# Every reciprocal square root as one GpSimd power, and another order of loads and work in the first norm of an encoder block

## The chip, the core and the metric

The kernel runs on one core of a Trainium2 chip. The metric is the device time of one execution in microseconds; a version's time is the median of its runs. TensorE multiplies matrices, VectorE, ScalarE and GpSimd (POOL in the profile) work on tiles of up to 128 partitions, and SyncE (SP) issues most of the transfers between the device's memory and the on-chip memory (SBUF; the matmul results land in PSUM).

## The reference, cut to what matters

```python
def rmsnorm(t, w, eps=1e-6):
    return t * lax.rsqrt(mean(t * t, -1) + eps) * w
h  = rmsnorm(x, norm1_w)                    # x: 1024 tokens x 1024
p  = h @ w_in                               # q/k/v, z, decay and beta logits, two gates
oa = diff_attention(rope(qa), rope(ka), va) # 8 heads, two softmaxes each, no mask
ya = rmsnorm(oa, subln_w) @ w_proj_attn     # norm over each head's 128 channels
qg, kg, vg = silu(conv5(qkv_g))             # centred, over the tokens
qg, kg = l2norm(qg), l2norm(kg)             # 8 heads of 128
o  = delta_rule(forward) + delta_rule(backward)   # chunks of 64 tokens
yg = (rmsnorm(o, gdn_norm_w) * silu(z)) @ w_proj_gdn
x  = x + (sigmoid(gate_a) * ya + sigmoid(gate_g) * yg) @ w_out
h2 = rmsnorm(x, norm2_w)
x  = x + expert_choice_ffn(h2)              # 16 experts, each takes its top 128 tokens
out = rmsnorm(x, norm_f_w)
```

Every `rsqrt` here, in the three norms, the head norms and the two l2norms, is a root that the change touches. All values are float32.

## The kernel before

The eight tiles of 128 tokens are normed, transposed by TensorE into the blocks `hh` and `hl` (each value as the sum of two that TensorE takes at its fast rate), and then a stream of tasks runs: the logit products of the gated delta rule (GDN below), its eight heads, the eight attention heads, the merge, the router, the sixteen experts, the last norm. Weights come in as float32 and are split the same way, ScalarE casting and GpSimd subtracting.

No order is written out by hand. Tasks are generators that record operations with a helper each: L391 is a product, L395 a transpose (both TensorE), L403 any ScalarE operation, L409, L428, L429 and L434 are VectorE's, L413 and L514 are GpSimd's products and scalar operations, L420 its memset, L483 a transfer. Each record has a planner cost in ns, and `run` takes, again and again, the operation that could start first by the planner's clocks, then by the task's priority. Each engine executes in the order so made. A change of one cost or one operation therefore plans everything behind it anew. Names in the rows are SBUF blocks (A, B, C, W with a number) or `psum`; small vectors lie in the C and B blocks.

A root is `rsqrt` (L528, eleven VectorE operations: an integer seed in two and three Newton steps of three) or, for seven of the eight router tiles, `prsqrt` (L516, two on VectorE and twelve on GpSimd). There are 45: eight of [128x1] in the first norm (`norm_tile`, L719), eight of [128x16] in the GDN heads (`Head.main`, L974), eight of [128x8] at the end of those heads (`Head.finish`, L1173; there the head's output is scaled, transposed and projected) and eight at the end of the attention heads (L1372), eight of [128x1] in the router (L1580), and five at the end: four of [128x2] for pairs of token tiles (`final_pair`, L1947) and one of [128x1] (L1886) for the tile whose rows the scatter waits for.

The first norm (`norm_first`, L753) asks SyncE for the norm's weights, the identity for the transposes and then the eight tiles of x, in that order. The mean square of a tile is a ScalarE square with an accumulator. Even tiles are scaled by root and weight in one VectorE operation, odd tiles by ScalarE (root) and GpSimd (weight). Eight transposes of a tile are evicted by ScalarE (`hh`), and VectorE takes the rest (`hl`, the "residual" below). A task `consts` records the constants' transfers at once, among them the convolution weights, which VectorE scales once.

At the very end the pairs of token tiles are normed while SyncE stores them, and odd tiles of the first three pairs are scaled by ScalarE and GpSimd.

Of the kernel before, what the change touches and what calls it, by code (L numbers as in the profile page):

```python
# [10 lines left out]
I32 = mybir.dt.int32  # L11
# [8 lines left out]
NT = S // P  # L20
# [14 lines left out]
def bcast(ap, shape):  # L35
    return ap.to_broadcast(shape)
# [72 lines left out]
class Emit:  # L109
# [405 lines left out]

    def prsqrt(self, y, x, t):  # L516

        i = t[:, 1].bitcast(I32)
        t = t[:, 0]
        self.ts(i, x.bitcast(I32), 1, op0=ALU.arith_shift_right)  # L520
        self.ts(y.bitcast(I32), i, -1.0, float(0x5F3759DF), op0=ALU.mult, op1=ALU.add)
        for _ in range(3):
            self.ptt(t, y, y, ALU.mult)
            self.ptt(t, t, x, ALU.mult)
            self.pts(t, t, -0.5, 1.5)
            self.ptt(y, t, y, ALU.mult)

    def rsqrt(self, y, x, t):  # L528

        i = t[:, 1].bitcast(I32)  # L530
        t = t[:, 0]
        self.ts(i, x.bitcast(I32), 1, op0=ALU.arith_shift_right)
        self.ts(y.bitcast(I32), i, -1.0, float(0x5F3759DF), op0=ALU.mult, op1=ALU.add)
        for _ in range(3):
            self.tt(t, y, y, ALU.mult)
            self.stt(t, t, -0.5, x, ALU.mult, ALU.mult)
            self.stt(y, t, 1.5, y, ALU.add, ALU.mult)

# [179 lines left out]

def norm_tile(g, st, w1):  # L719
    e = g.e  # L720
    xs = yield from e.new("xs", [P, D])
    e.dma(xs.v, g.ins["x"][st * P:(st + 1) * P, :])
    yield
    ss, rs = g.nsm[:, st:st + 1], g.nsm[:, 8 + st:9 + st]
    e.act(g.jk.v, xs.v, AF.Square, accum_out=ss)
    e.ts(ss, ss, 1.0 / D, 1e-6)
    e.rsqrt(rs, ss, g.nsm[:, 16 + 2 * st:18 + 2 * st].rearrange("p (a b) -> p a b", b=1))
    yield
    if st % 2:
        e.cp(xs.v, xs.v, scale=rs)  # L730
        e.ptt(xs.v, xs.v, w1.v, ALU.mult)
    else:
        e.stt(xs.v, xs.v, rs, w1.v, ALU.mult, ALU.mult)
    pt = yield from e.new("n0", [P, 8, P])
    for d in range(8):
        e.tr(pt[:, d, :], xs[:, d * P:(d + 1) * P], g.ident.v)
    yield
    o = slice(st * P, (st + 1) * P)
    e.cp(g.hh[:, :, o], pt.v)
    e.tt(g.hl[:, :, o], pt.v, f32(g.hh[:, :, o]), ALU.subtract)  # L740
    e.free(xs, pt)

    def done():
        g.tiles.add(st)
        g.hready[0] = g.tiles >= {0, 1, 2, 3}
        g.hready[1] = len(g.tiles) == 8
    e.then(done)
    if st == 7:
        e.free(w1, g.jk)
        e.close("xs", "w1", "n0", "jk")  # L750


def norm_first(g):  # L753
    e = g.e
    g.hT = e.now_new("hh", [P, 8, S], F32R), e.now_new("hl", [P, 8, S], F32R)
    g.hh, g.hl = g.hT[0].v, g.hT[1].v
    g.nsm = e.now_new("nsm", [P, 96]).v
    g.hready, g.tiles = [False, False], set()
    w1 = e.now_new("w1", [P, D])
    g.jk = e.now_new("jk", [P, D])  # L760
    e.spawn(norm_tile(g, 0, w1), 0)
    yield
    e.dma(w1.v, bcast(g.ins["norm1_w"], [P, D]))
    e.dma(g.ident.v, g.ins["c_ident"])
    for st in range(1, NT):
        e.spawn(norm_tile(g, st, w1), 0)
        yield
# [96 lines left out]
class Head:  # L864
# [81 lines left out]
    def main(self):  # L946
# [26 lines left out]
        e.ts(ss, ss, 1e-6, op0=ALU.add)  # L973
        e.rsqrt(rk, ss, rt)  # L974
        e.tt(irk, rk[:, 0:8], ss[:, 0:8], ALU.mult)
# [183 lines left out]
    def finish(self):  # L1159
# [12 lines left out]
        e.ts(m2, m2, 1.0 / 128, 1e-6)  # L1172
        e.rsqrt(rr, m2, rt)  # L1173
        e.tt(rr, rr, aq, ALU.mult)
# [50 lines left out]
class Attn:  # L1225
# [142 lines left out]
    def finish(self):  # L1368
        g, e, o, sm = self.g, self.g.e, self.o, self.sm
        ss, rr = sm[:, 0:8], sm[:, 8:16]  # L1370
        e.ts(ss, ss, 1.0 / 128, 1e-6)
        e.rsqrt(rr, ss, sm[:, 16:32].rearrange("p (a b) -> p a b", b=8))  # L1372
        e.tt(o.v, o.v, bcast(rr[:, :, None], [P, NT, P]), ALU.mult)
# [181 lines left out]
def router(g, st, xt, po):  # L1555
# [23 lines left out]
    e.ts(ss, ss, 1.0 / D, 1e-6)  # L1579
    (e.rsqrt if st == NT - 1 else e.prsqrt)(rs, ss, sm[:, 4:6].rearrange("p (a b) -> p a b", b=1))  # L1580
    pl = yield from e.new("gp", [P, 512])
# [152 lines left out]
class Experts:  # L1734
# [142 lines left out]
    def last(self, pd):  # L1877
# [7 lines left out]
        e.ts(ss, ss, 1.0 / D, 1e-6)  # L1885
        e.rsqrt(rs, ss, rt.rearrange("p (a b) -> p a b", b=1))  # L1886
        e.stt(x.v, x.v, rs, g.wf.v, ALU.mult, ALU.mult)
# [51 lines left out]
def final_pair(g, st, xs, fs):  # L1939
# [6 lines left out]
    e.ts(ss, ss, 1.0 / D, 1e-6)  # L1946
    e.rsqrt(rs, ss, fs[:, 16 + 2 * st:20 + 2 * st].rearrange("p (a b) -> p a b", b=2))  # L1947
    for i, x in enumerate(xs):
# [34 lines left out]
def body(tc, ins, out, dbg=None, heads=H):  # L1983
# [3 lines left out]
    with ExitStack() as ctx:  # L1987
# [170 lines left out]
```

## Time and profile before

| what | value |
|---|---|
| median of 3 runs | 3042.06 us (3036.37 to 3043.48) |
| the profiled execution | 3041.05 us |
| its span in the trace | 3039.3 us, 40711 instructions |
| TensorE products, weight loads | 2874.6 us (95%), 2401.8 us (79%) |
| VectorE, ScalarE, GpSimd | 2371.7 us (78%), 1752.0 us (58%), 567.5 us (19%) |
| TensorE's granted clock, mean | 0.981 of full speed |

Busy times are shares of the span; the engines work at the same time, so the shares don't add up. What remains of the execution's time beside its span is 1.75 us. Times of rows in the sections below count from the span's start.

### The profile page before, as it was taken

The numbers are of one execution on the slowest core, as the hardware profiler recorded it, in microseconds if no ns is written. First come the engines' busy times: TensorE is split into PE (matmuls) and PEld (weight loads), VectorE is DVE, ScalarE is ACT, GpSimd is POOL, SyncE is SP. The second block draws the span as 40 slices with busy tenths as digits, with TensorE's granted clock in tenths as the row PEclk, the third lists the DMA queues.
The fourth block names the chain that finished last, engine by engine and source line by source line (L and its number), as shares of the span: only waits on it lengthen the run. The fifth ranks groups of instructions, "written<-read, shape, count | busy, mean of one in ns | idle before, by whom it ended". The sixth has DMA issues, their size and how long they took to land.

```text
span 3039.3 us, 40711 instructions
## 1 busy us (share of the span) xinstructions
PE 2874.6 (95%) x14780; PEld 2401.8 (79%) x14780; DVE 2371.7 (78%) x3948; ACT 1752.0 (58%) x2668; POOL 567.5 (19%) x448
## 2 busy tenths in 40 slices
PE   7999999899998999999999997899999999999996
PEld 6787887788787878888888786788888888888884
DVE  7768778777865777777862458899888989989887
ACT  5435445444534666776662323577767777777775
POOL 3222222222212211211216332500000000000001
PEclk9999999999999999999999997899999999999998
DMA  4222322321322111112459736899999999999995
GB/s 139 52 68 83 84 61 60 90 63 52 89 74 61 49 49 49 49 49 56 112 161 290 231 105 246 311 390 378 372 386 381 380 383 377 378 377 381 373 355 235
DMA packets 203642, 598.75 MB, mean 197 GB/s; under 512 B 84384, under 2 KB 102304, under 8 KB 154288
## 3 DMA queue, kind: packets, MB, share of 16 engines
q1 hardware_dynamic: 189856, 562.06, 51.4%
q0 software_dynamic: 13584, 34.08, 4.0%
q8 instruction: 116, 1.90, 0.3%
q14 instruction: 86, 0.70, 0.1%
HBM read 535.19 MB, written 52.49 MB: 193 GB/s over the span
## 4 chain that ended last, share of the span: by engine, by line
PE 70%; DVE 15%; ACT 3%; DMA 3%; issue 3%; SPq 1%; POOL 1%; POOLq 0%; DVEq 0%; ACTq 0%
PE psum L391 66%; DVE B L409 6%; PE psum L395 4%; DVE B L434 4%; ACT B L403 2%; DVE B L451 2%; SPq L483 1%; ACT psum L403 1%; DMA dw<-B 1%; DVE B L428 1%; DVE B L455 0%; POOL W L413 0%; ACT W L403 0%; DMA A<-dh,C 0%; DMA B<-dl 0%
## 5 line engine op out<-in xcount | busy, mean ns | idle before, releaser
L391 PE MATMUL psum<-A,W 128*128 128x512 f32 (+1 forms) x5856 | 1548.6, 404 | 13.8 <-POOL W L413 5.5
L391 PEld LDWEIGHTS psum<-A,W 128*128 128x128 f32 (+1 forms) x5856 | 1068.0, 189 | 213.4 <-DVE A L409 10.2
L391 PE MATMUL psum<-B 128*128 128x128 f32 (+3 forms) x3494 | 651.6, 324 | 15.9 <-DVE B L455 7.6
L391 PEld LDWEIGHTS psum<-B 128*128 128x128 f32 x3494 | 544.8, 191 | 92.4 <-DVE B L455 11.1
L403 ACT ACTIVATE B<-psum 128x512 f32<-128x512 f32 (+4 forms) x612 | 266.4, 441 | 400.4 <-PE psum L395 225.3
L403 ACT ACTIVATE B<-B 128x2048 fp32r<-128x2048 f32 (+4 forms) x341 | 381.8, 1130 | 183.3 <-DVE B L434 80.8
L413 POOL TENSOR_TENSOR W<-W,W 128x1024 fp32r<-128x1024 f32 (+1 forms) x105 | 265.2, 2527 | 945.9 <-ACT W L403 818.1
L409 DVE TENSOR_TENSOR B<-B,B 128x2048 fp32r<-128x2048 f32 (+2 forms) x189 | 377.3, 2006 | 34.0 <-ACT B L403 27.1
L391 PE MATMUL psum<-B,W 128*128 128x512 f32 x1536 | 374.0, 395 | 4.0 <-DVE B L409 3.8
L391 PEld LDWEIGHTS psum<-B,W 128*128 128x128 f32 x1536 | 286.0, 189 | 74.2 <-DVE B L409 14.8
L403 ACT ACTIVATE B<-psum,B 128x128 f32<-128x128 f32 (+2 forms) x264 | 190.9, 728 | 197.4 <-PE psum L391 124.7
L395 PE MATMUL psum<-C,B 128*128 128x128 f32 (+1 forms) x1392 | 218.9, 281 | 71.7 <-DVE B L434 28.3
L409 DVE TENSOR_TENSOR A<-B,A 128x2048 fp32r<-128x2048 f32 x112 | 256.7, 2306 | 15.6 <-ACT A L403 14.5
L391 PE MATMUL psum<-A,B 128*128 128x512 f32 x1024 | 264.5, 398 | 2.3 <-DVE A L409 2.3
L395 PEld LDWEIGHTS psum<-C,B 128*128 128x128 f32 (+1 forms) x1392 | 170.6, 144 | 120.7 <-DVE B L434 35.0
L403 ACT ACTIVATE A<-B 128x2048 fp32r<-128x2048 f32 (+1 forms) x121 | 222.7, 1857 | 41.4 <-PE psum L391 20.6
L391 PE MATMUL psum<-B,B 128*128 128x128 f32 (+1 forms) x1024 | 212.6, 294 | 13.7 <-DVE B L460 11.5
L391 PEld LDWEIGHTS psum<-A,B 128*128 128x128 f32 x1024 | 191.0, 189 | 40.5 <-DVE A L409 3.0
L391 PEld LDWEIGHTS psum<-B,B 128*128 128x128 f32 x1024 | 175.4, 192 | 40.9 <-DVE B L460 14.8
L497 POOL DMA_INDIRECT dx<-B,C x15 | 24.3, 1618 | 953.9 <-ACT B L403 953.9
L451 DVE TENSOR_REDUCE B<-psum 128x1 f32<-128x1024 f32 (+1 forms) x136 | 157.3, 1158 | 53.9 <-PE psum L391 53.0
L413 POOL TENSOR_TENSOR B<-B,B 128x128 f32<-128x128 f32 (+3 forms) x98 | 131.6, 1346 | 308.6 <-ACT B L403 218.8
(116 smaller groups left out, 2852.6 us busy)
## 6 DMA issues: line engine op xcount, KB each, us to landing
B<-in_w_gu_dram SPq DMA_DIRECT2D x154, 1024.0 KB, 7.3
A<-in_w_gu_dram SPq DMA_DIRECT2D x77, 1024.0 KB, 7.3
B<-in_w_dn_dram SPq DMA_DIRECT2D x74, 1024.0 KB, 7.3
A<-in_w_dn_dram SPq DMA_DIRECT2D x40, 1024.0 KB, 7.6
W<-in_w_gu_dram SPq DMA_DIRECT2D x25, 1024.0 KB, 7.1
W<-in_w_gdn_dram SPq DMA_DIRECT2D x32, 512.0 KB, 3.7
B<-dG SPq DMA_DIRECT2D x32, 512.0 KB, 5.6
W<-in_w_proj_dram SPq DMA_DIRECT2D x32, 512.0 KB, 4.6
```

The source lines that it names most:

```text
L391: self.op("pe", c, lambda: self.nc.tensor.matmul(out, lhsT, rhs, start=start, stop=stop), [out], [lhsT, rhs], l, "mm")
L395: self.op("pe", 109, lambda: self.nc.tensor.transpose(out, in_, ident), [out], [in_, ident], 55, "tr")
L403: self.op("act", c, lambda: self.nc.scalar.activation(out, in_, func, **kw), [out] + w, [in_] + r, 0, "act")
L409: self.op("dve", 69 + 1.041 * free(out), lambda: self.nc.vector.tensor_tensor(out, a, b, op), [out], [a, b], 0, "tt")
L413: self.op("pool", 150 + 2.104 * free(out), lambda: self.nc.gpsimd.tensor_tensor(out, a, b, op), [out], [a, b], 0, "ptt")
L428: lambda: (self.nc.vector.tensor_scalar(out, a, s1, None, op0=op0) if s2 is None else self.nc.vector.tensor_scalar(out, a, s1, s2, op0=op0 ...
L434: lambda: self.nc.vector.scalar_tensor_tensor(out, a, s, b, op0=op0, op1=op1),
L451: self.op("dve", 69 + 1.041 * free(in_), lambda: self.nc.vector.tensor_reduce(out, in_, axis=AX.X, op=op), [out], [in_], 0, "red")
L483: self.op("sp", 478, lambda: self.nc.sync.dma_start(out, in_), [out], [in_], 0, "dma", max(n / 360.0, 112))
L497: self.op("pool", 1100, lambda: self.nc.gpsimd.indirect_dma_start(out=dst, out_offset=bass.IndirectOffsetOnAxis(ap=idx, axis=0), in_=y, in ...
```

## The change

`prsqrt` and the old `rsqrt` go. The new `rsqrt` is one GpSimd operation, x to the power of a column that holds -0.5, with a planner cost of 150 + 20n ns for n columns; the column is set once, at the start. The first norm asks for tile 0 of x first, then the identity, the norm's weights and the other tiles; all eight tiles are scaled by VectorE; the constants are asked for only when two tiles are done (by then the logit weights and the first projection weights are in the queue ahead of them).

```diff
-    def prsqrt(self, y, x, t):
...
-    def rsqrt(self, y, x, t):
-        i = t[:, 1].bitcast(I32)
-        t = t[:, 0]
-        self.ts(i, x.bitcast(I32), 1, op0=ALU.arith_shift_right)
-        self.ts(y.bitcast(I32), i, -1.0, float(0x5F3759DF), op0=ALU.mult, op1=ALU.add)
-        for _ in range(3):
-            self.tt(t, y, y, ALU.mult)
-            self.stt(t, t, -0.5, x, ALU.mult, ALU.mult)
-            self.stt(y, t, 1.5, y, ALU.add, ALU.mult)
+    def rsqrt(self, y, x):
+        n = free(x)
+        h = self.half[:, 0:1] if n == 1 else bcast(self.half[:, 0:1], [P, n])
+        self.op("pool", 150 + 20 * n, lambda: self.nc.gpsimd.tensor_tensor(y, x, h, op=ALU.pow), [y], [x, self.half], 0, "pow")
...
-def norm_tile(g, st, w1):
+def norm_tile(g, st, w1, xs):
     e = g.e
-    xs = yield from e.new("xs", [P, D])
-    e.dma(xs.v, g.ins["x"][st * P:(st + 1) * P, :])
-    yield
     ss, rs = g.nsm[:, st:st + 1], g.nsm[:, 8 + st:9 + st]
     e.act(g.jk.v, xs.v, AF.Square, accum_out=ss)
     e.ts(ss, ss, 1.0 / D, 1e-6)
-    e.rsqrt(rs, ss, g.nsm[:, 16 + 2 * st:18 + 2 * st].rearrange("p (a b) -> p a b", b=1))
+    e.rsqrt(rs, ss)
     yield
-    if st % 2:
-        e.cp(xs.v, xs.v, scale=rs)
-        e.ptt(xs.v, xs.v, w1.v, ALU.mult)
-    else:
-        e.stt(xs.v, xs.v, rs, w1.v, ALU.mult, ALU.mult)
+    e.stt(xs.v, xs.v, rs, w1.v, ALU.mult, ALU.mult)
...
     w1 = e.now_new("w1", [P, D])
+    e.pset(e.half, -0.5)
     g.jk = e.now_new("jk", [P, D])
-    e.spawn(norm_tile(g, 0, w1), 0)
-    yield
-    e.dma(w1.v, bcast(g.ins["norm1_w"], [P, D]))
-    e.dma(g.ident.v, g.ins["c_ident"])
-    for st in range(1, NT):
-        e.spawn(norm_tile(g, st, w1), 0)
+    for st in range(NT):
+        xs = yield from e.new("xs", [P, D])
+        e.dma(xs.v, g.ins["x"][st * P:(st + 1) * P, :])
+        if st == 0:
+            e.dma(g.ident.v, g.ins["c_ident"])
+            e.dma(w1.v, bcast(g.ins["norm1_w"], [P, D]))
+        e.spawn(norm_tile(g, st, w1, xs), 0)
         yield
...
         def consts():
+            yield lambda: len(g.tiles) > 1
             for n, shp in (("neg", [P, 2, P]), ("eye16", [P, 256]), ("m16", [P, 2, P]), ("m32", [P, 2, P])):
```

Every other caller only loses the scratch argument.

How the order of the engines moves, at the start and at the last GDN head. On ScalarE at the start, `B_81,C_76<-B_80` is a square of an x tile with its accumulator, `A_78<-psum` the eviction of a tile's transposes, `B_80<-B_80,C_76` the scaling of an odd tile, and `W_111<-W_83` (`W_99` after) the cast of the logit weights (128x256) and of the first projection weights (128x1024). Before:

```order
L403 ACTIVATE B_81,C_76<-B_80 128x1024 x5
L403 ACTIVATE A_78<-psum 128x8x128
L403 ACTIVATE B_80<-B_80,C_76 128x1024
L403 ACTIVATE B_81,C_76<-B_80 128x1024 x2
L403 ACTIVATE A_78<-psum 128x8x128
L403 ACTIVATE B_80<-B_80,C_76 128x1024
L403 ACTIVATE A_78<-psum 128x8x128
L403 ACTIVATE B_81,C_76<-B_80 128x1024
L403 ACTIVATE W_111<-W_83 128x256
L403 ACTIVATE W_111<-W_83 128x1024
```

And after:

```order
L403 ACTIVATE B_81,C_76<-B_80 128x1024 x2
L403 ACTIVATE A_78<-psum 128x8x128
L403 ACTIVATE B_81,C_76<-B_80 128x1024 x2
L403 ACTIVATE A_78<-psum 128x8x128
L403 ACTIVATE B_81,C_76<-B_80 128x1024 x2
L403 ACTIVATE A_78<-psum 128x8x128
L403 ACTIVATE B_81,C_76<-B_80 128x1024
L403 ACTIVATE A_78<-psum 128x8x128
L403 ACTIVATE B_81,C_76<-B_80 128x1024
L403 ACTIVATE W_99<-W_83 128x256
L403 ACTIVATE W_99<-W_83 128x1024
```

The scalings of odd tiles are gone from ScalarE, and four evictions instead of three stand ahead of the logit weights. On TensorE at the same place, L395 `psum<-C_76,B_80` are transposes of x tiles, eight to a tile, and L391 the logit products. Before:

```order
L395 MATMUL psum<-C_76,B_80 128x128 x24
L391 MATMUL psum<-A_78,W_111 32x256
L395 MATMUL psum<-C_76,B_80 128x128 x16
L391 MATMUL psum<-A_79,W_111 32x256
L391 MATMUL psum<-A_78,W_111 32x256 x2
```

And after:

```order
L395 MATMUL psum<-C_76,B_80 128x128 x40
L391 MATMUL psum<-A_78,W_99 32x256
L391 MATMUL psum<-A_79,W_99 32x256
L391 MATMUL psum<-A_78,W_99 32x256 x2
L391 MATMUL psum<-A_79,W_99 32x256
```

Five tiles are transposed ahead of all logit products, where one such product stood among them. On VectorE the scaling of the convolution weights now stands between the scaling of a sixth tile and the fifth tile's residual. The other place is VectorE at the end of the last GDN head (`Head.finish`): the 128x8 rows are the mean square and the root, `B_80<-B_80,B_82 128x1024` the scaling of the head's output, `B_7778<-B_82,B_7778 64x1024` residuals of projection weights (`B_7524` after), and `B_82<-B_82,B_80` and `B_80<-B_80` of 128x1024 belong to attention. Before, from the mean's last step on:

```order
L429 TENSOR_SCALAR B_82<-B_82 128x8
L428 TENSOR_SCALAR B_82<-B_82 128x8
L429 TENSOR_SCALAR B_82<-B_82 128x8
L409 TENSOR_TENSOR B_82<-B_82 128x8
L434 SCALAR_TENSOR_TENSOR B_82<-B_82 128x8
L409 TENSOR_TENSOR B_7778<-B_82,B_7778 64x1024 x2
...
L409 TENSOR_TENSOR B_82<-B_82,B_80 128x1024
L409 TENSOR_TENSOR B_80<-B_80 128x1024
L434 SCALAR_TENSOR_TENSOR B_82<-B_82 128x8
L409 TENSOR_TENSOR B_82<-B_82,B_80 128x1024
...
L409 TENSOR_TENSOR B_80<-B_80,B_82 128x1024
```

And after:

```order
L428 TENSOR_SCALAR B_82<-B_82 128x8
L409 TENSOR_TENSOR B_82<-B_82 128x8 x2
L429 TENSOR_SCALAR B_82<-B_82 128x8
L409 TENSOR_TENSOR B_82<-B_82 128x8
L409 TENSOR_TENSOR B_7524<-B_82,B_7524 64x1024 x2
L409 TENSOR_TENSOR B_80<-B_80,B_82 128x1024
```

The steps of the root and the three attention products between them are gone from the stretch; the two residuals still stand ahead of the scaling.

## Rows read from the trace of the kernel before

**Rows 1.** Stages: us, busy (instructions) PE, PEld, DVE, ACT, POOL; PEclk, DMA share, GB/s.
```profile
0.00:44.70 44.70, 25.40 (x170) 22.37 (x170) 27.59 (x110) 25.49 (x37) 14.66 (x10) 0.92 0.48 164
44.70:960.00 915.30, 863.59 (x4910) 737.43 (x4909) 681.19 (x1973) 408.88 (x1149) 224.45 (x194) 0.99 0.26 71
...
1976.00:2980.00 1004.00, 1003.58 (x4539) 818.83 (x4538) 901.04 (x550) 736.15 (x508) 40.08 (x28) 1.00 0.98 377
2980.00:3040.00 60.00, 31.42 (x129) 24.10 (x127) 44.39 (x83) 27.32 (x31) 10.15 (x4) 0.79 0.52 211
```

**Rows 2.** Timeline, first 13 us: start, us, instruction [idle before, releaser].
```profile
0.75 0.39 SPq L483 DMA_DIRECT2D B<-in_norm_w_dram  x1
...
8.11 1.06 ACT L403 ACTIVATE B<-B 128x1024 f32<-128x1024 f32 x1 [6.09 <-DMA B<-in_x_dram]
...
11.61 1.28 DVE L434 SCALAR_TENSOR_TENSOR B<-B,C 128x1024 f32<-128x1024 f32 x1
...
12.96 1.97 PE L395 MATMUL psum<-C,B 128*128 128x128 f32 x8 [12.96 <-DVE B L434]
```

**Rows 3.** Timeline from 13 us to the first projection (last three: TensorE's alone).
```profile
13.23 0.33 SPq L483 DMA_DIRECT2D C<-in_conv_w_dram  x1
...
14.96 1.02 ACT L403 ACTIVATE A<-psum 128x1024 fp32r<-128x1024 f32 x1 [0.52 <-PE psum L395]
...
17.10 2.36 POOL L413 TENSOR_TENSOR B<-B 128x1024 f32<-128x1024 f32 x1 [16.64 <-ACT B L403]
...
20.62 1.14 ACT L403 ACTIVATE B<-B,C 128x1024 f32<-128x1024 f32 x1
...
21.84 3.24 POOL L413 TENSOR_TENSOR B<-B 128x1024 f32<-128x1024 f32 x1 [2.38 <-ACT B L403]
...
23.60 1.36 ACT L403 ACTIVATE W<-W 128x256 fp32r<-128x256 f32 x2
...
25.18 3.67 PE L395 MATMUL psum<-C,B 128*128 128x128 f32 x16 [0.81 <-DVE C L409]
28.50 5.21 PE L391 MATMUL psum<-A,W 128*32 128x256 f32 x32
...
44.69 9.59 PE L391 MATMUL psum<-A,W 128*128 128x512 f32 x41
```

**Rows 4.** Timeline at the end of the last GDN head.
```profile
973.87 0.17 DVE L429 TENSOR_SCALAR B<-B 128x8 f32<-128x8 f32 x1
...
974.88 2.47 DVE L409 TENSOR_TENSOR B<-B,B 64x1024 fp32r<-64x1024 f32 x2
...
984.39 7.85 DVE L409 TENSOR_TENSOR B<-B,B 128x1024 f32<-128x1024 f32 x3
...
985.67 1.11 PE L395 MATMUL psum<-C,B 128*128 128x128 f32 x4 [8.79 <-DVE B L409]
```

**Rows 5.** TensorE's waits from 76 to 1000 us: total us, times, longest.
```profile
PE psum L395 <- DVE B L409: 19.1, 6, 8.8
```

**Rows 6.** Chain that ended last, from 2985 to 3040 us, by line.
```profile
by line: issue 24.3%; DVE B L409 18.8%; DVE B L434 8.0%; DVE C L434 7.2%; ACT B L403 5.6%; DMA out_dram<-B 4.8%; DVE C L429 3.8%; DVE C L409 3.7%; PE psum L391 2.9%; DVE A L434 2.5%; POOLq L2154 2.2%; DVE C L428 1.3%; PE psum L395 0.8%; DVE
```

**Rows 7.** GpSimd's instructions by form: count | busy us, mean ns | idle before, releasers.
```profile
L413 POOL TENSOR_TENSOR W<-W,W 128x1024 fp32r<-128x1024 f32 x104 | 264.5, 2544 | 945.9 <-ACT W L403 818.1 <-PE psum L391 86.0 <-PE psum L395 27.3
...
L413 POOL TENSOR_TENSOR B<-B 128x1 f32<-128x1 f32 x63 | 12.0, 191 | 67.3 <-DVE B L429 62.8
```

**Rows 8.** Timeline at a router root made on GpSimd.
```profile
1842.66 0.13 DVE L429 TENSOR_SCALAR B<-B 128x1 int32<-128x1 int32 x1
...
1842.93 0.46 POOL L413 TENSOR_TENSOR B<-B 128x1 f32<-128x1 f32 x2 [8.23 <-DVE B L429]
...
1846.13 0.17 DVE L451 TENSOR_REDUCE B<-psum 128x1 f32<-128x16 f32 x1 [0.41 <-PE psum L391]
```

**Rows 9.** Transfers issued in the first 60 us: count, KB each, us to landing.
```profile
B<-in_norm_w_dram SPq DMA_DIRECT2D x1, 512.0 KB, 4.4
...
C<-in_conv_w_dram SPq DMA_DIRECT2D x1, 60.0 KB, 5.5
```

More of the change, by code (lines that the diff above doesn't have):

```diff
@@ L514, in pts @@
                          self.nc.gpsimd.tensor_scalar(out, a, s1, s2, op0=op0, op1=op1)), [out], [a], 0, "pts")
-    def prsqrt(self, y, x, t):
-        i = t[:, 1].bitcast(I32)
-        t = t[:, 0]
-        self.ts(i, x.bitcast(I32), 1, op0=ALU.arith_shift_right)
-        self.ts(y.bitcast(I32), i, -1.0, float(0x5F3759DF), op0=ALU.mult, op1=ALU.add)
-        for _ in range(3):
[L523 to L526, printed above, removed]
-    def rsqrt(self, y, x, t):
[L530 to L534, printed above, removed]
-            self.tt(t, y, y, ALU.mult)
-            self.stt(t, t, -0.5, x, ALU.mult, ALU.mult)
-            self.stt(y, t, 1.5, y, ALU.add, ALU.mult)
+    def rsqrt(self, y, x):
+        n = free(x)
+        h = self.half[:, 0:1] if n == 1 else bcast(self.half[:, 0:1], [P, n])
+        self.op("pool", 150 + 20 * n, lambda: self.nc.gpsimd.tensor_tensor(y, x, h, op=ALU.pow), [y], [x, self.half], 0, "pow")
 class Ctx:
@@ L973, in main @@
         e.ts(ss, ss, 1e-6, op0=ALU.add)
-        e.rsqrt(rk, ss, rt)
+        e.rsqrt(rk, ss)
         e.tt(irk, rk[:, 0:8], ss[:, 0:8], ALU.mult)
@@ L1172, in finish @@
         e.ts(m2, m2, 1.0 / 128, 1e-6)
-        e.rsqrt(rr, m2, rt)
+        e.rsqrt(rr, m2)
         e.tt(rr, rr, aq, ALU.mult)
@@ L1371, in finish @@
         e.ts(ss, ss, 1.0 / 128, 1e-6)
-        e.rsqrt(rr, ss, sm[:, 16:32].rearrange("p (a b) -> p a b", b=8))
+        e.rsqrt(rr, ss)
         e.tt(o.v, o.v, bcast(rr[:, :, None], [P, NT, P]), ALU.mult)
@@ L1579, in router @@
     e.ts(ss, ss, 1.0 / D, 1e-6)
-    (e.rsqrt if st == NT - 1 else e.prsqrt)(rs, ss, sm[:, 4:6].rearrange("p (a b) -> p a b", b=1))
+    e.rsqrt(rs, ss)
     pl = yield from e.new("gp", [P, 512])
@@ L1885, in last @@
         e.ts(ss, ss, 1.0 / D, 1e-6)
-        e.rsqrt(rs, ss, rt.rearrange("p (a b) -> p a b", b=1))
+        e.rsqrt(rs, ss)
         e.stt(x.v, x.v, rs, g.wf.v, ALU.mult, ALU.mult)
@@ L1946, in final_pair @@
     e.ts(ss, ss, 1.0 / D, 1e-6)
-    e.rsqrt(rs, ss, fs[:, 16 + 2 * st:20 + 2 * st].rearrange("p (a b) -> p a b", b=2))
+    e.rsqrt(rs, ss)
     for i, x in enumerate(xs):
@@ L2006, in body @@
         g.one = e.now_new("one", [P, 64])
+        e.half = g.one[:, 63:64]
         g.logits = g.gdn_done = g.gdn_close = g.attn_ok = g.routes = g.route0 = g.list1 = g.rank_ok = False
```

## The prediction

> **What bounds the kernel now.** I read the stages first [rows 1]. From 1976 to 2980 us TensorE is busy 1003.58 of 1004 us and holds no root but those of the last few microseconds: that stretch can only be started earlier. Before it TensorE idles where a chain of small steps ends last: 19.3 us in the first 44.7 (44.70 less 25.40), 51.7 in the heads' stretch to 960 (915.30 less 863.59). In the last 60 us it idles 28.6.
>
> Then the timeline of each place that holds a root. *Start* [rows 2]: x tile 0 is the third transfer; its square begins at 8.11, the eleven small VectorE steps of its root end at 11.61, where the scaling begins, and its transposes begin at 12.96. From 28.50 [rows 3] TensorE has no gap that matters: the 16 transposes from 25.18 were the last to wait, then logit products and the other 24 transposes run on until the first head's projection starts at 44.69. So 28.50 is the moment that has to move, not the end of the norm. *Last GDN head* [rows 4]: the mean square is ready at 973.87 + 0.17, but the scaling by the root is the first of the three VectorE products that begin at 984.39, and TensorE, whose next instruction is the transpose of what it gives, waits 8.79 us. Over all heads TensorE lost 19.1 us, six times, in this kind of wait [rows 5]. *Tail* [rows 6]: in the chain that ended last, from 2985 us, the small VectorE operations on C (7.2 + 3.8 + 3.7 + 1.3 %) are 16% of 55 us, 8.8 us.
>
> **What a power costs.** No row shows one. Below, it is the [128x1] GpSimd product, 191 ns [rows 7]: the same form, less arithmetic. Above, it is the root that GpSimd now makes by hand in twelve instructions, from 1842.93 to just before 1846.13, 3.2 us [rows 8]. How it grows with columns is just as open: a product grows from 191 ns at one column to 2.54 us at 1024 (2.3 ns per column) [rows 7]; at worst every column costs a whole 3.2. The new function tells the scheduler 150 + 20n ns, which nobody has measured here; it lies at the low end, near the product, the nearest row in form, and I take that side: about 0.2, 0.3 and 0.5 us for 1, 8 and 16 columns, plus 0.14 for the step from VectorE to GpSimd (a VectorE step ending at 1842.66 + 0.13, GpSimd starting at 1842.93 [rows 8]) and 0.1 back, a guess.
>
> **The start.** Tile 0 takes the place of the norm weights, which land 4.4 us after an issue at 0.75 [rows 2, 9]: square from 5.2, mean at 6.6, power done by 7.2. The weights are now third and land where x did, 8.0. So the scaling runs from about 8.1, 3.5 us earlier, its transposes from 9.5 to 11.5 at the 1.97 us of now. ScalarE then runs, by the order shown, four evictions (1.02 each [rows 3]) and six squares (1.06 [rows 2], about 1.17 with the read of the accumulator) from 11.8 to 22.9 before it casts the logit weights; it no longer has two scalings of 1.14 ahead of that cast, which was at 23.60, and GpSimd splits the cast weights with no x product of 3.24 before it [rows 3]. Logits begin at about 24.2. Five tiles' transposes are then behind TensorE, just as at 28.50 now, with the same work left. That took 16.2 us (44.69 less 28.50), so the projections start at about 40.4: **4.3 us**.
>
> Two things could spoil it. VectorE gives up 80 of the 88 tiny steps of the start and takes four more scalings of 1.28 [rows 2]: eight scalings and eight residuals of that size, 20.5 us from 8.1, and little beside them, end near 30, and the last logit products need them only at 36 (40.4 less the 5 us or so of the last logits). And the constants, asked for later, put a new wait ahead of the fifth tile's residual on VectorE: the scaling of the convolution weights, in its in-order queue. From the norm weights at 0.75 to these at 13.23 there are fourteen issues [rows 2, 3], 0.9 us each; two more go ahead of them now (logit weights and a first projection weight), so they go out at about 15.0 and take some 5.5 [rows 9]: 20.5. VectorE's own work up to that point, six scalings and four residuals, ends at 8.1 + 12.8, about 21 to 22. That residual is needed by about 28, so the wait has some 6 us of cover. Bounds from the clock: 0.92 granted over the start [rows 1] means about 7 of its 44.7 us at the 1.2 GHz level and the rest at 2.4; none of that gives back 3.6 us, twice that takes 3.6. So 0.7 to 7.9.
>
> **The GDN heads.** At the last head the order keeps only two residuals of 64x1024 (2.47 us together [rows 4]) between the mean and the scaling: 973.87 + 0.17 + 0.6 for the power and its two hand-overs + 0.17 for the next small product + 2.47 = 977.3; with the scaling's 1.3 that is 978.6, where it was 985.67. TensorE runs out of other work at 985.67 less 8.79, 976.88, so 8.79 becomes 1.7, a gain of 7.1; I book **6**, since GpSimd's weight splits (2.54 [rows 7]) stand in the same queue. The other five waits sum to 10.3 (19.1 less 8.8 [rows 5]); the scheduler plans each transpose against the shorter chain, so much of a shorter chain is planned away into an earlier place: I book **3**, bounds 0 and 10.3. Of the sixteen-column roots, the one of head 0 has no earlier head's work beside it: eleven steps 0.2 apart (five of them from 973.87 to 974.88 [rows 4]) are 2.2, less a power of 0.5 and 0.24 of hand-overs: **1.5**. The other seven are hidden by the head before: 0.
>
> **Router and attention.** The seven GpSimd roots shrink from 3.2 to 0.2, but the reduction after one, at 1846.13, was released by TensorE [rows 8]: the logits end last there, so **0**. Attention's eight roots have other rows' work around them: 0, and at most 2 for one that has none.
>
> **The tail.** Of 8.8 us five mean steps and five powers stay (5 x 0.17 + 5 x 0.42 = 2.9): 5.9 at most. But pair 2's power stands behind pair 0's GpSimd product (2.36 for such a one), itself behind a ScalarE scaling (1.14 [rows 3]), and VectorE's next steps queue behind it. The scatter also still waits for eight stores. I take half, **3**.
>
> Sum: 4.3 + 6 + 3 + 1.5 + 3 = 17.8 off the profiled execution's own 3041.05 (span 3039.3 and 1.75 around it): 3023.3; the median lies 1.0 above that execution, so **3024**.
>
> **A code load at the first power.** The first GpSimd product now runs at 17.10 in 2.36 us [rows 3], no longer than the 2.54 of later ones [rows 7], so no load shows in a span, but the 16.64 idle microseconds ahead could hide one. If 6 us fell on tile 0's power it would end near 13, ScalarE's in-order eviction would be about five later, the logits would begin at 28.5 as now, and the 4.3 would be gone: 3028. The Trainium skill, "GPSIMD Engine Reference", section 2.1 (Instruction dispatch), says that the first call to a freshly loaded GpSimd kernel pays about 6 us that no instruction shows (5.95 measured). By it the sum is 3028 if the load waits for the first power, 3024 if it comes with the preparatory instruction that stands ahead of that power and waits for nothing. No row here separates the two.
>
> **Rivals.** *No change*: the whole order behind the first norm is planned anew, the terms that rest on where a step stands (6 + 3 + 1.5 + 3) go, 4.3 stays: 3038. For it: 51.7 us of idle in the heads' stretch come from many small waits that move with any plan. Against it: the 8.79 is the work of eleven steps and what was queued between them, and those eleven leave VectorE. *Slower, GpSimd's queue*: a power stands in order behind a weight split that waits for its ScalarE cast; 104 splits waited 818.1 us for casts, about 8 each [rows 7]. Two such waits on the path of a head's root take back 16 of the 17.8; five of sixteen, 39 us, give 3063. Against it: the scheduler issues whatever can start first, and a split is issued late. *Slower, power by columns*: at 0.5 us per column the sixteen-column root is 8.2 us instead of 2.2, +48 over eight heads, less the 4.3 of the start: some 3085 if all is exposed, 3070 with a third hidden; it decides from about 0.3 per column. Against it: GpSimd's slope of 2.3 ns.
>
> **How the numbers follow.** A measurement of this kernel tells about 0.3% (9 us) from nothing. Forecast 0.58 (3010 to 3033), code load 0.08 (3028), no change 0.20 (3038), queue 0.08 (3063), power by columns 0.06 (3070). Faster 0.66, same 0.20, slower 0.14. The upper ends (7.9 at the start, 7.1 and 10.3 at the finishes, 1.5, 5.9) give 3009, and an exposed attention root or two 3006; the range runs from there to 3044, past the no-change case, and leaves out the slow ones.
>
> **What the changed profile would show.** Powers of one column near 0.2 us, of sixteen near 0.5; tile 0's square near 5.2; logits without a gap from about 24 and the first 128x512 product near 40; a wait of TensorE before the last head's transposes under 3 us; the stretch of full TensorE as long as now. I am wrong if a power costs microseconds, if GpSimd's powers wait behind splits, or if the heads' idle grows by more than the places above give.

## The result and the profile after

The changed kernel takes **3068.29 us** (3066.6 to 3069.85, four runs) against 3042.06 before: 1.0089 of the time, 95% interval 1.0074 to 1.0104. It is slower by some 27 us, where 18 us faster was forecast. The profiled execution took 3067.89 us. (One execution of a kernel of the next section, the order with 68 ns, took 3589.6 us at a mean granted clock of 0.75, and its time is given without it.) First the page's span and busy times, then three stages (columns as in [rows 1]; the first ends where the first projection starts):

```profile
span 3066.1 us, 40223 instructions
PE 2892.5 (94%) x14780; PEld 2406.2 (78%) x14780; DVE 2316.0 (76%) x3520; ACT 1745.7 (57%) x2664; POOL 606.8 (20%) x406
```

```profile
0.00:38.70 38.70, 25.25 (x170) 22.03 (x170) 20.65 (x26) 21.13 (x33) 9.54 (x15) 1.00 0.54 189
38.70:960.00 921.30, 855.47 (x4768) 723.04 (x4768) 651.70 (x1784) 402.36 (x1136) 258.88 (x208) 0.98 0.25 69
...
2000.00:3004.00 1004.00, 1003.58 (x4541) 818.75 (x4541) 900.32 (x552) 733.30 (x508) 40.47 (x28) 1.00 0.98 377
```

VectorE loses 428 instructions and 55.7 us of work, and the kernel is slower. The start is shorter by 6.0 us, and its mean granted clock is 1.00 where it was 0.92 [rows 1]; the stretch of full TensorE is as long as before (1003.58 of 1004). What is lost lies between 38.7 us and the experts. The timeline of the start, which answers to [rows 2, 3]:

```profile
4.39 1.06 ACT L403 ACTIVATE B<-B 128x1024 f32<-128x1024 f32 x1 [2.38 <-DMA B<-in_x_dram]
...
5.89 0.57 POOL L520 TENSOR_TENSOR C<-C 128x1 f32<-128x1 f32 x1 [5.06 <-DVE C L429]
...
7.24 1.28 DVE L434 SCALAR_TENSOR_TENSOR B<-B,C 128x1024 f32<-128x1024 f32 x1 [1.50 <-DMA B<-in_norm_w_dram]
...
8.58 1.97 PE L395 MATMUL psum<-C,B 128*128 128x128 f32 x8 [8.58 <-DVE B L434]
...
23.72 1.59 PE L391 MATMUL psum<-A,W 128*32 128x256 f32 x7 [0.51 <-POOL W L413]
...
38.67 9.59 PE L391 MATMUL psum<-A,W 128*128 128x512 f32 x41
```

Each step stands about where the prediction put it, a little earlier. The power of tile 0 is done at 6.46, and the scaling waits for the weights. What a power costs is in GpSimd's groups by form (columns as in [rows 7]):

```profile
L520 POOL TENSOR_TENSOR B<-B,C 128x8 f32<-128x8 f32 x16 | 27.2, 1700 | 146.7 <-DVE B L429 131.3 <-DMA dgate<-W 15.3
...
L520 POOL TENSOR_TENSOR B<-B,C 128x16 f32<-128x16 f32 x8 | 24.2, 3022 | 94.2 <-DVE B L428 94.2
...
L520 POOL TENSOR_TENSOR B<-B,C 128x1 f32<-128x1 f32 x8 | 4.4, 553 | 89.3 <-DVE B L429 89.3
...
L520 POOL TENSOR_TENSOR C<-C,C 128x2 f32<-128x2 f32 x4 | 2.8, 702 | 36.5 <-DVE C L429 36.4
```

0.55 us for one column, 0.70 for two, 1.70 for eight, 3.02 for sixteen: close to 0.4 us and 0.157 us per column, where the scheduler is told 0.15 and 0.02. These are means: of the eight powers of sixteen columns the first took 3.88 us and the others 2.89 to 2.92. Nearly all of the idle time before the powers ended with a value from VectorE, and GpSimd stood idle before each of the 24 in the heads, so these did not queue. Who waited for them, in VectorE's waits (total us, times, longest):

```profile
DVE B L409 <- POOL B L520: 36.6, 20, 3.0
...
DVE C L409 <- POOL B L520: 6.4, 4, 1.8
```

These 43.0 us are new. How one of them comes about, at the first head, whose power is the longest:

```profile
85.54 0.17 DVE L428 TENSOR_SCALAR B<-B 128x16 f32<-128x16 f32 x1 [0.29 <-ACT psum L403]
...
85.79 3.88 POOL L520 TENSOR_TENSOR B<-B,C 128x16 f32<-128x16 f32 x1 [4.20 <-DVE B L428]
...
89.71 0.24 DVE L409 TENSOR_TENSOR B<-B 128x8 f32<-128x8 f32 x2 [2.81 <-POOL B L520]
...
91.60 0.30 PEld L391 LDWEIGHTS psum<-B 128*128 128x128 f32 x2 [2.61 <-DVE B L409]
```

VectorE stands still for 2.81 us in front of a 128x8 product that needs the power, with everything behind it in its queue, and then TensorE waits too. At the end of the last GDN head, which answers to [rows 4], the power takes 1.64 us where 0.3 was reckoned; TensorE waits 3.91 us where it waited 8.79. The row of four is two residuals, the scaling and an attention product behind it; the second residual is shown by itself too, with the GpSimd weight split beside it:

```profile
992.40 0.17 DVE L429 TENSOR_SCALAR B<-B 128x8 f32<-128x8 f32 x1
992.65 1.64 POOL L520 TENSOR_TENSOR B<-B,C 128x8 f32<-128x8 f32 x1 [11.44 <-DVE B L429]
...
994.52 6.91 DVE L409 TENSOR_TENSOR B<-B,B 64x1024 fp32r<-64x1024 f32 x4
995.15 2.81 POOL L413 TENSOR_TENSOR W<-W,W 128x1024 fp32r<-128x1024 f32 x1 [0.86 <-ACT W L403]
995.77 3.27 DVE L409 TENSOR_TENSOR B<-B,B 64x1024 fp32r<-64x1024 f32 x1
...
1000.35 0.66 PE L395 MATMUL psum<-C,B 128*128 128x128 f32 x4 [3.91 <-DVE B L409]
```

The two residuals that the order has are still the only ones ahead of the scaling, but the second took 3.27 us where the first took 1.22 (994.52 to 995.74): it began while the split ran and ended 1.08 us after the split. So did all 21 residuals of this size that began under a split in the traces before and after; the 43 others took 1.22 or 1.23. No VectorE instruction that began while a power ran was held up like this (30 in the trace after, none more than 12% over its usual time).

In the router [rows 8] the power of 0.55 us is off the path, and the reduction after the logits is released by TensorE as before:

```profile
1888.01 0.55 POOL L520 TENSOR_TENSOR B<-B,C 128x1 f32<-128x1 f32 x1 [11.84 <-DVE B L429]
...
1891.51 0.17 DVE L451 TENSOR_REDUCE B<-psum 128x1 f32<-128x16 f32 x1 [1.63 <-PE psum L391]
```

The chain that ended last in the last 55 us, which answers to [rows 6]:

```profile
by line: PE psum L391 22.2%; DMA B<-dx 21.2%; DVE A L409 8.2%; issue 6.4%; DVE B L409 5.4%; DVE A L434 4.9%; DMA out_dram<-B 4.7%; POOL C L520 4.1%; DVE B L434 3.4%; POOLq L2134 2.3%; DVEq L2134 2.2%; SPq L483 2.1%; DVE C L429 0.2%; POOLq L
```

The small VectorE steps on C, 16% of it before, are 0.2%, and the powers take 4.1%.

To see in which stage the time went, transfers that every version makes serve as marks: the last store of a GDN head's output (`dog`), the last of an attention head's (`doa`), the first scatter of an expert (into `dx`) and the last of the eight reads of `dx` for the last norm. Of the kernel before, then of the one after (number of issues: shortest, median, longest ns, first to last start):

```profile
L483 SPq DMA_DIRECT2D dog<-B x64: 319/322/672, 242.8 to 1002.9; - x64
...
L483 SPq DMA_DIRECT2D doa<-C x64: 319/326/952, 1091.2 to 1611.2; - x64
```

```profile
L483 SPq DMA_DIRECT2D dog<-B x64: 319/320/655, 242.0 to 1023.0; - x64
...
L483 SPq DMA_DIRECT2D doa<-C x64: 319/322/809, 1110.7 to 1634.4; - x64
```

Read in this way from the profiled execution of each version (us; the last two marks are at 1988.6 and 2988.5 before, 2020.5 and 3021.0 after; the kernels from the third row on are experiments of the next section):

| kernel | start | GDN heads | attention | merge, router | experts | tail | span |
|---|---|---|---|---|---|---|---|
| before | 44.7 | 958.2 | 608.3 | 377.4 | 999.9 | 50.8 | 3039.3 |
| after | 38.7 | 984.3 | 611.4 | 386.1 | 1000.5 | 45.1 | 3066.1 |
| start alone | 40.6 | 955.4 | 605.6 | 378.4 | 999.9 | 48.4 | 3028.3 |
| small roots alone | 40.9 | 955.8 | 608.6 | 377.3 | 1000.1 | 45.5 | 3028.2 |
| after, true cost | 38.9 | 960.5 | 607.3 | 394.1 | 1000.4 | 45.2 | 3046.4 |
| its order, short stand-ins | 39.1 | 954.3 | 601.0 | 396.7 | 999.8 | 45.4 | 3036.3 |
| after's order, short stand-ins | 38.2 | 945.0 | 607.4 | 385.9 | 1000.3 | 45.2 | 3022.0 |
| before, 66 for 69 | 44.2 | 970.2 | 622.6 | 386.8 | 999.5 | 48.5 | 3071.8 |

The start gains 6.0 and the tail 5.7; the GDN heads lose 26.1, merge and router 8.7, attention 3.1. The marks are in the middle of work that any order shifts between stages, so a difference of a few microseconds in one stage can stand in the next. And a row is one execution, which can lie some microseconds off its kernel's median: 3048.15 us against 3044.01 for the true cost, 3038.14 against 3041.52 for its order with short stand-ins.

### The profile page after: what moved, and what is told of

The parts are those of the page before. It is cut to its first block, busy times and chain, and to the rows that moved or that the text cites. A ratio compares the mean times of both kernels' runs of the same rounds, so it can differ in the third digit from the quotient of the medians.

```text
span 3066.1 us, 40223 instructions
## 1 busy us (share of the span) xinstructions
PE 2892.5 (94%) x14780; PEld 2406.2 (78%) x14780; DVE 2316.0 (76%) x3520; ACT 1745.7 (57%) x2664; POOL 606.8 (20%) x406
## 5 line engine op out<-in xcount | busy, mean ns | idle before, releaser
L391 PE MATMUL psum<-A,W 128*128 128x512 f32 (+1 forms) x5856 | 1554.4, 405 | 11.5 <-POOL W L413 5.8
L391 PEld LDWEIGHTS psum<-A,W 128*128 128x128 f32 (+1 forms) x5856 | 1069.3, 190 | 211.4 <-POOL W L413 9.8
L391 PE MATMUL psum<-B 128*128 128x128 f32 (+3 forms) x3494 | 655.7, 325 | 29.3 <-DVE B L455 14.0
L391 PEld LDWEIGHTS psum<-B 128*128 128x128 f32 x3494 | 548.7, 192 | 112.7 <-DVE B L455 20.5
L391 PE MATMUL psum<-B,W 128*128 128x512 f32 x1536 | 374.4, 395 | 4.0 <-DVE B L409 3.7
L391 PEld LDWEIGHTS psum<-B,W 128*128 128x128 f32 x1536 | 285.9, 189 | 74.6 <-DVE B L409 15.2
L395 PE MATMUL psum<-C,B 128*128 128x128 f32 (+1 forms) x1392 | 222.3, 284 | 60.2 <-DVE B L409 23.3
L391 PE MATMUL psum<-A,B 128*128 128x512 f32 x1024 | 266.2, 399 | 1.4 <-DVE A L409 1.4
L395 PEld LDWEIGHTS psum<-C,B 128*128 128x128 f32 (+1 forms) x1392 | 172.7, 145 | 111.3 <-DVE B L434 36.8
L403 ACT ACTIVATE A<-B 128x2048 fp32r<-128x2048 f32 (+1 forms) x121 | 222.6, 1857 | 40.9 <-PE psum L391 19.5
L391 PE MATMUL psum<-B,B 128*128 128x128 f32 (+1 forms) x1024 | 211.7, 294 | 21.3 <-DVE B L460 18.6
L391 PEld LDWEIGHTS psum<-A,B 128*128 128x128 f32 x1024 | 190.2, 189 | 39.2 <-DVE A L409 2.4
L391 PEld LDWEIGHTS psum<-B,B 128*128 128x128 f32 x1024 | 174.6, 192 | 50.1 <-DVE B L460 24.3
L451 DVE TENSOR_REDUCE B<-psum 128x1 f32<-128x1024 f32 (+1 forms) x136 | 157.1, 1157 | 45.7 <-PE psum L391 43.8
```

The costliest lines, as they stand in the source:

```text
L391: self.op("pe", c, lambda: self.nc.tensor.matmul(out, lhsT, rhs, start=start, stop=stop), [out], [lhsT, rhs], l, "mm")
L395: self.op("pe", 109, lambda: self.nc.tensor.transpose(out, in_, ident), [out], [in_, ident], 55, "tr")
L403: self.op("act", c, lambda: self.nc.scalar.activation(out, in_, func, **kw), [out] + w, [in_] + r, 0, "act")
L451: self.op("dve", 69 + 1.041 * free(in_), lambda: self.nc.vector.tensor_reduce(out, in_, axis=AX.X, op=op), [out], [in_], 0, "red")
```

## The experiments

Three theories stood against each other. **A**: the powers of 8 and 16 columns take 1.4 and 2.5 us longer than the scheduler is told, so the order that it makes has nothing under them. **B**: such a root is simply a longer chain on GpSimd, whatever is told. **C**: any new order moves the time by tens of microseconds, and the change only drew another one. Ratios are to the kernel before in runs on the same chip.

**Which part of the change.** The start alone: the new first norm, with the old functions back for the other 37 roots; and the roots alone: the new `rsqrt` everywhere with the old `norm_tile`, `norm_first` and `consts`.

```diff
 # start alone, against after; likewise at the five other callers
-        e.rsqrt(rk, ss)
+        e.vrsqrt(rk, ss, rt)     # the eleven VectorE steps
 # roots alone, against after, and norm_tile and norm_first as before
...
-            yield lambda: len(g.tiles) > 1
```

> The new first norm alone: power for its eight [128x1] roots, tile 0 asked for first, VectorE scaling, late constants; all other 37 roots as in the kernel before. The first projection starts at 38.7 us, as after the change. Theory A (the scheduler is told 150 + 20n ns for a power that takes 0.55 to 2.9 us, so VectorE is queued behind it in the heads) and theory B (a root of 8 or 16 columns is simply a longer chain on GpSimd) both say that what was lost is in the other roots: 6.0 us faster than before, 3036. Theory C (any new plan of the order moves the time by tens of us, and the old plan was a good draw): anywhere from 3025 to 3070. If the late constants do the harm: 3060 or more.

Measured: 3034.18 us, ratio 0.9981 (0.9970 to 0.9992). Behind the start TensorE's order is that of the kernel before (by names and shapes 32 of 14780 products stand elsewhere, the last at 34.5 us), so this run is no new draw.

> The power for all 45 roots, with the loads, the scaling of odd tiles and the constants of the first norm as in the kernel before. A and B: the heads lose their 26 us as after the change and the start gains little: 3068 to 3076. C: no bound to the one side, 3040 to 3075, and another distribution of losses over the heads.

Measured: 3067.57 us, ratio 1.0085 (1.0063 to 1.0107). VectorE waits 36.5 us, 20 times, for powers, as after the change. That is 0.4 us under the range of A and B. The loss is in the roots, and the late constants do no harm. Against after, 22 of TensorE's products stand elsewhere, all in the first 32 us: no new draw either. In the order of the start alone the first projection starts at 40.55, 4.1 earlier than before; the rest of its 5.9 (by the medians) comes later.

**Small roots alone.** Powers for the roots of one or two columns, told at their true price; the 24 of 8 and 16 columns on VectorE.

```diff
-        self.op("pool", 150 + 20 * n, ...
+        self.op("pool", 395 + 157 * n, ...
 # and e.vrsqrt in Head.main, Head.finish and Attn.finish
```

> The new first norm, and powers only where a root has one or two columns: first norm, router, last norm, told at 395 + 157n; the 24 roots of 8 and 16 columns in both kinds of heads on VectorE as before the change. A and B: the start's 6 and the tail's 5.7 (the last part went from 50.8 us after the last read of an expert's rows to 45.1) come together: 3028 to 3032, a few us under the run with the start alone (3034). If the powers of the router or of the tail cost anything: 3036 or more.

Measured: 3030.09 us, ratio 0.9967 (0.9954 to 0.9979). Of the versions that compute every root it has the lowest median, though its interval overlaps that of the start alone; both beat both kernels. Against the start alone its tail is 2.9 us shorter.

**The order, with no root changed.** The kernel before, with one planner cost changed by 3, 1, 1 and 3 ns.

```diff
-        self.op("dve", 69 + 1.041 * free(out), lambda: self.nc.vector.tensor_tensor(out, a, b, op),
+        self.op("dve", 72 + 1.041 * free(out), lambda: self.nc.vector.tensor_tensor(out, a, b, op),
```

> The kernel before, all roots as they were; only the planner's base cost of a VectorE product is 72 ns in place of 69, so that no operation changes and the order is planned anew. A and B: 3042, within 5. C: the time moves by more than 10, up or down, most likely up, 3050 to 3075.

Measured with 72: 3044.84 us, ratio 1.0018 (1.0007 to 1.0029), as A and B have it.

> The kernel before with a planner base cost of 66 ns in place of 69 for a VectorE product, the other side of the run with 72 (+5). If a new order alone moves the time by some 10 or 20 us: outside 3030 to 3050. If its scatter is about 5: 3035 to 3045.

Measured with 66: 3074.91 us, ratio 1.0106 (1.0085 to 1.0126). A and B had nothing to say on this, C had: the same operations in another order cost 33 us, more than the whole change.

> The kernel before with a planner base cost of 70 ns in place of 69 for a VectorE product. If 3042 is a usual draw: 3035 to 3050, as with 72. If it is a lucky one: 3050 to 3080, as with 66.

Measured with 70: 3051.72 us, ratio 1.0038 (1.0024 to 1.0052).

> The same with 68 ns. Usual draw: 3035 to 3050. Lucky: 3050 to 3080.

Measured with 68: 3052.51 us, ratio 1.0034 (1.0020 to 1.0048). Four draws of four are slower than the kernel before, by 5 to 33 us; in each, 3600 to 4200 of TensorE's 14780 products stand elsewhere. So a difference of 27 us proves nothing on the powers by itself; what the powers cost has to be measured in an order that stays.

**Telling the truth.** The changed kernel with 395 + 157n in place of 150 + 20n, and, meant as a control, a cost moved by 10 ns that is still wrong.

> The changed kernel with a planner cost of 395 + 157n ns, the line through the measured powers (0.55 us at 1 column, 0.70 at 2, 1.67 at 8, 2.9 at 16), in place of 150 + 20n. A: the scheduler puts other VectorE work ahead of what waits for a power, the 36.6 us that VectorE waited for powers fall under 15, and 15 to 25 us come back: 3043 to 3053. B: little comes back, 3060 to 3070. C: anywhere from 3035 to 3075, without a tie to the waits for powers.

Measured: 3044.01 us, ratio 1.0007 (0.9996 to 1.0017). VectorE's waits for powers, in the row that had 36.6 and 20, and the one that had 6.4 and 4:

```profile
DVE B L409 <- POOL B L520: 9.6, 7, 1.9
...
DVE C L409 <- POOL B L520: 3.3, 2, 1.8
```

> The changed kernel with a planner cost of 160 + 20n ns for a power: a new plan that is still as wrong on the slope (157 measured). A: 3063 to 3073, and VectorE still waits 30 us or more for powers. C (the 24 us that the true cost gave back are only another draw): as likely near 3044 as near 3068.

Measured with 160 + 20n: 3062.62 us, ratio 1.0079 (1.0056 to 1.0101), and the waits are again 36.6 us, 20 times. The first came out as A has it, the second 0.4 us under A's range. But the second is not the new order that it was meant to be: row by row its trace has after's order on VectorE and GpSimd, and differs in six rows on ScalarE and 60 of TensorE's products, nearly all in the first 33 us. So it says nothing against C; what separates A from C is the orders held still below.

**One form at a time.** The [128x16] roots back on VectorE, then instead the [128x8] roots at the end of the GDN heads; each once told wrong and once told right.

```diff
 # against after: the first run, and the second
-        e.rsqrt(rk, ss)
+        e.vrsqrt(rk, ss, rt)
...
-        e.rsqrt(rr, m2)
+        e.vrsqrt(rr, m2, rt)
```

> The changed kernel with the eight [128x16] roots of the GDN heads back on VectorE in eleven steps; the other 37 stay powers, told to the scheduler as 150 + 20n. What the scheduler is not told is 2.4 us for each of these (2.9 less 0.47) and 1.4 us for each of the sixteen [128x8] powers (1.67 less 0.31). A: this form holds the larger part of the heads' loss of 26 us, some 15 of it: 3053, range 3045 to 3060. If these powers are harmless: 3065 or more. C: not tied to the form.

Measured: 3059.96 us, ratio 1.0067 (1.0050 to 1.0084), at the upper end of A's range.

> The changed kernel with the eight [128x8] roots at the end of the GDN heads back on VectorE; the other 37 stay powers, told as 150 + 20n. A: the smaller part, some 8 us: 3060, range 3053 to 3066. If the loss is all in this form: under 3050.

Measured: 3083.97 us, ratio 1.0145 (1.0128 to 1.0162). Eight long powers fewer, VectorE's waits for powers down from 43.0 to 32.4 us, and 16 us slower: outside what A allowed.

> The run at 3084 with the true planner cost, 395 + 157n. A: telling the truth gives back here too what it gave back in the changed kernel (24): 3060 or less, and more likely about 3045, since only 16 head roots are powers. C: no tie, 3045 to 3090.

Measured: 3044.23 us, ratio 1.0014 (1.0004 to 1.0023), as A has it.

> The run at 3060 (the [128x16] roots on VectorE, the others powers) with the true planner cost. A: 3045 or less; with the start's 6 and the tail's 3 to 6 and harmless [128x8] powers it would be 3030 to 3036, as with powers for the small roots alone (3030). If the [128x8] powers cost something even when told right: 3038 to 3048.

Measured: 3041.78 us, ratio 1.0013 (1.0003 to 1.0022). Told right, all three mixtures lie at 3042 to 3044, whether 16 or 24 head roots are powers; so what is left over 3030 doesn't follow the powers' number.

**Holding the order still.** The planner's costs, and with them every engine's order, stay as they are; only what runs on the chip in the 24 head roots becomes short.

```diff
-        self.op("pool", 150 + 20 * n, lambda: self.nc.gpsimd.tensor_tensor(y, x, h, op=ALU.pow), ...
+        short = n > 2
+        if short:
+            h = bcast(self.tiny, [P, n])     # a column of 1e-4
+        self.op("pool", 150 + 20 * n, lambda: self.nc.gpsimd.tensor_tensor(y, x, h, op=ALU.mult if short else ALU.pow), ...
...
 # in norm_first, one more memset: the column of 1e-4
```

> The changed kernel, told the same 150 + 20n, so that the order of every engine is that of the changed kernel row for row; but in the 24 roots of 8 and 16 columns (both kinds of heads) a GpSimd product with a small constant stands in the power's place, which is about as short as the scheduler was told. The head roots are left out of the result by this, and one more memset stands at the start. If the time that the powers really take is what cost 26 us (A and B): 30 us or so come back, 3030 to 3045, and VectorE waits under 10 us for them. If the new order is worse by itself, whatever the powers take (C): 3060 to 3068.

Measured: 3023.06 us, ratio 0.9951 (0.9936 to 0.9966). Row by row the traces have the same order on every engine, but for the memset. The stand-ins by form, and VectorE's waits for them:

```profile
L523 POOL TENSOR_TENSOR B<-B,C 128x8 f32<-128x8 f32 x16 | 4.2, 264 | 145.8 <-DVE B L429 138.8 <-DMA dgate<-W 7.0
L523 POOL TENSOR_TENSOR B<-B,C 128x16 f32<-128x16 f32 x8 | 2.7, 339 | 94.2 <-DVE B L428 94.2
```

```profile
DVE B L409 <- POOL B L523: 1.7, 5, 0.4
DVE C L409 <- POOL B L523: 0.9, 3, 0.3
```

The 24 powers took 27.2 + 24.2 = 51.4 us, the stand-ins 6.9: 44.5 less. VectorE's waits fall from 43.0 to 2.6, and the time falls by 45.2 us by the medians, 42 by the two ratios. So about as much reached the end as the powers were shortened by. It is not all waiting: in the GDN heads TensorE's stage rows, after and then with stand-ins, are

```profile
38.70:1023.00 984.30, 913.24 (x5064) 771.72 (x5063) 687.48 (x1838) 425.85 (x1187) 277.13 (x215) 0.98 0.25 69
```

```profile
38.20:983.20 945.00, 896.53 (x5065) 761.87 (x5063) 687.15 (x1838) 425.54 (x1187) 244.66 (x215) 0.99 0.26 72
```

Of the 39.3 us between them 22.6 are idle time of TensorE (71.1 less 48.5) and 16.7 are longer busy time in the same order, at a mean granted clock of 0.98 against 0.99. The stand-ins also change the values that later work gets; that this isn't what gave the time back is shown by the last run of this section, where the same stand-ins give back 2.5.

> The order of the run at 3063 (160 + 20n), row for row, with short stand-ins in the 24 head roots (left out of the result; one more memset at the start). The 24 powers take some 51 us in all, the stand-ins some 7. If that is exposed nearly one to one in any order planned for short powers, as in the two orders tried: 3015 to 3028. If those two were special: 3040 or more.

Measured: 3023.95 us, ratio 0.9952 (0.9934 to 0.9969): 38.7 us less than the same order with powers (3062.62). As that order is nearly after's, this repeats the run before and is no second order.

> The same stand-in in the order of the run at 3084 (the roots at the end of the GDN heads on VectorE, the other 37 told as 150 + 20n): the 16 roots of 16 and 8 columns that were powers there are short products now, so those roots are left out. If the powers' duration made that 3084: 3045 or less. If that order is a bad one by itself: 3070 or more. In between: both, in that share.

Measured: 3050.32 us, ratio 1.0045 (1.0028 to 1.0062): 33.7 less than with powers (3083.97), where the sixteen powers took 38.3 us and the stand-ins 5.3, 33.0 less. This order does differ from after's (4741 of TensorE's products stand elsewhere), so the powers' duration is exposed nearly one to one in a second order too. What is left, 27 us over after's order with stand-ins, is the order and the eight roots of eleven VectorE steps together, which were not told apart; it is why the run with the fewer powers was the slower one.

> The kernel with the true planner cost (3044), its order row for row, with the short stand-in product in the 24 roots of 8 and 16 columns (those roots are left out of the result; one more memset at the start). If the powers' real duration is still on the path in that order: 3025 to 3035, 10 to 20 back. If the true cost has moved other work under them and the rest is the order's: 3040 to 3046.

Measured: 3041.52 us, ratio 0.9999 (0.9987 to 1.0010), against 3044.01 with the powers. Here the stand-ins give back 2.5 us only, which the two intervals (some 3 us to each side) don't tell from nothing: told right, the scheduler puts other work under the powers (VectorE waited 12.9 us for them, not 43.0), and they cost next to nothing. What keeps that version 15 to 18 us (by the ratios, by the medians) over after's order with stand-ins is its order. So B is out; A holds for what the powers cost, and C for what an order costs.

## Why the prediction was wrong

**The step that failed is the price of a power** ("I take that side: about 0.2, 0.3 and 0.5 us for 1, 8 and 16 columns"). The bounds held the truth, 0.55, 1.70 and 3.02, but the forecast was made with the lower one, because the nearest row in form, the product at 191 ns [rows 7], was taken for the nearest in price; the other bound, the hand-made root, was a chain of twelve instructions and was passed over, though it was the only row of the same function. With head roots about as short as assumed, after's own order is at 3023, where 3024 was forecast (partly by luck, as said below). What the sum left out is the rest of the price: 44.5 us more work in the 24 head roots, and 42 to 45 us at the end.

**"The other seven are hidden by the head before: 0"** failed with it. Between after and its order with stand-ins the GDN heads differ by 39.3 us; their sixteen powers are longer than the stand-ins by 33.0 (24.2 less 2.7, and half of 27.2 less 4.2). On balance none was hidden, since the order had been made for roots that need no cover. In attention it is 4.0 of 11.5. The new function's 150 + 20n had been read as a hint at the duration; it was an instruction to the scheduler, and its error was the loss: told right, 24 of the 27 us are gone.

**The rival that came true** is the power by columns, at a chance of 0.06. Its cause, a length that grows by columns, and its place were right; its price was 0.16 us per column, half of the 0.3 from which it was said to decide. The point of decision was too high because it reckoned only with the sixteen-column roots, against the 2.2 us of the old chain, and not with the cover that a wrong cost takes away, nor with the sixteen roots of eight columns. By its own sum a power of 2.9 us against 2.2 loses 6 us over eight heads; that its 3070 lies near the measured 3068 is luck.

**GpSimd's queue** was not it: the head powers found GpSimd idle. **No change** (3038) did not come, but what stands behind it weighs more than the prediction gave it: a rest planned anew moved this kernel by 5 to 33 us for a nanosecond or three of one cost, as much as the terms of the sum and more. That the stand-in run meets the forecast is partly luck of this kind: by stages, after's order with stand-ins gains 6.5 at the start (4.3 booked), 13.2 in the GDN heads (10.5 booked), 0.9 in attention (0), 5.6 in the tail (3), and loses 8.5 in merge and router, which no term had.

**The terms that were right.** The start: 6.0, in its bounds of 0.7 to 7.9; the square came at 4.39 (5.2), the first projection at 38.67 (40.4), and the mean granted clock was 1.00, the case of the upper bound; with the start alone it was 0.92 as before, and the gain 4.1, where 4.3 was booked. (VectorE gives up all 88 root steps of the start, not 80, which changes nothing here.) The tail: 5.7 of at most 5.9, but some 2 of it are not the roots': the five other profiled kernels with the old roots there have tails of 48.4 to 48.8, those with powers 45.1 to 45.7, so the roots gave about the 3 booked. Pair 2's power did stand behind pair 0's product; it cost nothing, for the chain that ended last runs through a transfer there (DMA B<-dx). The router: 0, for powers alone in the small roots leave merge and router at 377.3 (377.4 before); the 8.7 lost there after the change is there with stand-ins too (8.5). The last GDN head: 4.9 of the 6 booked. It was not the queue that took from it: the power took 1.64 us, and a weight split held up a residual by 2.05 (3.27 less 1.22). **The code load** did not fall on the first power: it started at 5.89, 0.16 us after the mean, and took 0.57. The Trainium skill, "GPSIMD Engine Reference", section 2.1 (Instruction dispatch), has about 6 us for the first call of a fresh kernel; here nothing of it is seen at that call, and whether it was paid in the five idle microseconds ahead of it no run here shows.

Two things stay open. What makes one order up to 33 us worse than another was not traced to single waits. And of the 26.8 us by which the span grew, 8.9 are idle time of TensorE (173.6 after, 164.7 before, span less busy time) and 17.9 are more busy time of the same 14780 products. The mean granted clock was 0.980 after, 0.981 before and 0.985 in after's order with stand-ins; how much of the longer busy time is the clock's was not measured apart.

## What to carry to other kernels

A planner's cost is part of the kernel: here an operation that was told five or six times too short cost about its whole error in time (42.7 us untold, 42 to 45 lost), and told right next to nothing. Measure a new operation at each of its sizes before it goes into the cost table, and where the nearest rows lie far apart (0.2 us by form, 3.2 by function; 0.55 was true), carry both through the sum instead of choosing one. Where a change plans the order anew, run the old kernel with a cost moved by a nanosecond or two first, and look in the trace whether the order did move: that scatter is what a difference has to beat, and an order held still with a stand-in in the disputed place shows what the operation itself costs.

## What was not expected of the hardware

GpSimd's power grows by 0.157 us per column (0.55 at one, 3.02 at sixteen, on 128 partitions), while the product of the same form took 0.19 us at one column, 0.26 at eight and 0.34 at sixteen. A few powers took some 1 us more than the others of their form: two of [128x1] 1.54 us for 0.55 (at 14.09 and 3050.74 us in the trace after), the first of [128x16] 3.88 for 2.90; what those have in common was not tested. And a VectorE residual that began under a GpSimd weight split ended 1.08 us after the split, 21 times of 21, whatever was left of the split, while VectorE's work beside a power ran as usual.
